# High and low halves of q and k: one full-width copy and one difference, pieces placed by DMA, and later due times for q

## The chip, the cores and the metric

The kernel runs on one core of a Trainium2 chip. Its engines work side by side, each through its own list of instructions: TensorE (PE; its weight loads are shown as PEld), VectorE (DVE), ScalarE (ACT), GpSimd (POOL) and SyncE (SP), which here issues all DMAs. The metric is device time in microseconds; lower is better. A time is the median of several runs; a profile comes from one further execution, whose own time is given beside it.

## The reference

A network of four layers over 1040 tokens (16 meta tokens and 1024 of the input) with 1024 channels, in float32. Layers 0 and 3 are the same kind, sliding-window attention; layer 1 is an mLSTM and layer 2 an HGRN2. Only the attention layers are touched:

```python
def attention_branch(u, w_in, q_gain, k_gain, sinks, w_out, valid, pos):
    q, k, v, z = _split(u @ w_in, (A_W, A_KVW, A_KVW, A_W))
    q = rope(rmsnorm(q.reshape(bsz, lp, A_HEADS, A_HD), q_gain), pos)
    k = rope(rmsnorm(k.reshape(bsz, lp, A_KV, A_HD), k_gain), pos)
    v = v.reshape(bsz, lp, A_KV, A_HD)
    o = sliding_window_attention(q, k, v, sinks, valid)
    return (o * jax.nn.silu(z)) @ w_out

def reference(...):
    for i in range(DEPTH):
        u = rmsnorm(h, norm_gain[i])
        y = attention_branch(...) | mlstm_branch(...) | hgrn2_branch(...)
        h = h + where(valid, y, 0)
```

There are 16 query heads and 4 key heads of 64 channels; a token attends to itself and the 127 before it.

## The kernel before

Activations lie with channels on the 128 partitions and tokens along the free axis. The tokens come in three chunks of 400, 384 and 256 (`CHUNKS`; in layer 3 the first chunk of q is 384 wide, `LAST_CHUNKS`), and the attention in nine blocks, of 16 tokens and then of 128. To keep float32 accuracy with a fast matmul format, each operand is held as two rounded parts, high and low: `h = round(x)`, `l = x - h`. Weights and normed activations take three matmuls for each product (h·h, h·l, l·h).

Two heads share a tile of 128 partitions, 64 each. The scores use that: a q operand (`qs`) of one head has the high part in one half of its 128 partitions and the low part in the other, and k has two operands per head, one with the high part in both halves and one with the low part in both. So two matmuls (lines 621 and 622) give all four products. Building these operands is the split. Before, `k_split` (lines 432 to 451) makes, for each of two heads of a chunk, two copies of the high part (444, 445), one difference (446) and one copy of it (447). `q_split` (lines 453 to 470) makes one copy (463) and one difference (464) for each head. All of these work on 64 partitions, ACT the copies and DVE the differences, and write from one half of the partitions to the other where the operand asks for it.

What precedes a split is in `qk_proj`: the projection of one tile and chunk is 24 matmuls (line 228); `evac` (489) has ACT write the scaled values `dst` (492) and their squares `sq` (493) and has SP issue four DMAs of 32 partitions (496) that put the rotated quarters of `dst` into `rot`. Then come, at due times behind the projection: the rope table (`factors`, 503, one buffer); the statistic, a PE matmul over `sq` (516 for q, 525 for k); the rope itself, `dst*cos + rot*sin` (530 to 532), with the norm factor for k (534); and the split.

There are 8 q tiles per layer, so 8 x 3 splits of q in a layer and 48 in the kernel; there are two k tiles, so 2 x 3 splits of k in a layer, 12 in the kernel. `dst`, `sq` and `rot` of q, and of the second k tile, are three of six shared temporaries (`tmp()`, `TMPS = 6`), which v's evacuation, the gates and the norm units use too; the first k tile uses long rows instead. A temporary comes free when the last instruction or DMA that touches it is done. The norm units (386, 194, 195) make the two parts of the normed activations, tile by tile, ahead of the projections.

PE's order is written out by hand. Every step has a PE cost in ns, and `chain`, `spread` and `weave` merge the projections (fill) with the steps of the attention (S scores, T transposes, V values). The due times `D_K` and `D_Q` are in ns of PE work of the fill after a projection's end: for q the table, the statistic, the rope and the split; for k the statistic, the rope and the split. A step with no PE cost has only a place in the program; the other engines' and SP's lists are made by a scheduler that goes by that order and by what is ready. Each engine works through its list in order, and SP too: a DMA that has to wait for its data keeps back what stands behind it. Weights are loaded ahead by 12000 ns of PE work (`LOOKAHEAD`), into two raw buffers, and split by ACT and DVE (194, 195).

A layer starts with a head: for each chunk the first k tile and q tile 0 (in layer 0 also q tile 1; in layer 3 all three chunks of q tile 1 follow at the end). Then come four segments, one per pair of q tiles, with fill woven in: v and the next pair's q in the first, the second k tile, its v, gates and the last pair's q in the third, which runs 12000 ns (`K_AHEAD`) of fill before its scores. At the end of `layer_a` (748 to 754) a q split that would come before the last scores of the previous pair for its chunk is moved behind them, since `qs` has four buffers per chunk.

Of the kernel before, what the change touches and what calls it, by code (L numbers as in the profile page):

```python
# [9 lines left out]
F32 = mybir.dt.float32  # L10
F32R = mybir.dt.float32r
AF = mybir.ActivationFunctionType
ALU = mybir.AluOpType
PSUM = bass.MemoryType.PSUM

P = 128
# [8 lines left out]
CHUNKS = [(0, 400), (400, 384), (784, 256)]  # L25
# [4 lines left out]
def blk(b):  # L30
    return (0, NMETA) if b == 0 else (NMETA + P * (b - 1), P)
# [15 lines left out]
PARTS = 4  # L47
FIRST = (0.2, 0.8, 0.85), (0.2, 0.75, 0.8)
D_K = 2000.0, 4000.0, 6000.0
D_Q = 1500.0, 2500.0, 3500.0, 4500.0  # L50


MM = 1.0 / 2.4
# [58 lines left out]
def hybrid_kernel(ctx: ExitStack, tc: tile.TileContext, ins, out, layers=(0, 1, 2, 3)):  # L112
    nc = tc.nc
    v, s, g, pe, sp = nc.vector, nc.scalar, nc.gpsimd, nc.tensor, nc.sync
# [11 lines left out]
    def nm(x):  # L126
        ctr[0] += 1
        return f"{x}{ctr[0]}"
# [4 lines left out]
    def rrow():  # L133
        return rpool.tile([P, T], F32R, tag="r", name=nm("r"), bufs=ROWS)
# [16 lines left out]
    def psa():  # L151
        return psum("pa", 1)
# [58 lines left out]
    def proj(src, evac, chunks=CHUNKS):  # L211
        st = {}

        def pre():
            st["w"] = weights(src, "m")

        groups = []
        for n, (c0, cn) in enumerate(chunks):
            grp = []
            for part in range(4):  # L220
                def fn(n=n, c0=c0, cn=cn, part=part):
                    if part == 0:
                        st[n] = psj()
                    h, l = st["w"]
                    acc = st[n]
                    for k in (2 * part, 2 * part + 1):
                        for i, (a, b) in enumerate(((h, uh), (h, ul), (l, uh))):
                            pe.matmul(acc[:, :cn], a[:, k, :], b[:, k, c0 : c0 + cn],  # L228
                                      start=(k == 0 and i == 0), stop=(k == KT - 1 and i == 2))
                    if part == 3:  # L230
                        evac(acc, n, c0, cn)

                grp.append([6 * cn * MM, fn, pre if (n == 0 and part == 0) else None])
            groups.append(grp)
        return groups
# [101 lines left out]
    def rstd_from(acc, dst, cn, n):  # L337
        s.activation(dst[:, :cn], acc[:, :cn], AF.Ln, bias=eps, scale=1.0 / n)
        s.activation(dst[:, :cn], dst[:, :cn], AF.Exp, scale=-0.5)
# [76 lines left out]
    def layer_a(i, j, first, last, fin):  # L416
        win, wout = ins["a_win"][j], ins["a_wout"][j]
        chunks = LAST_CHUNKS if last else CHUNKS
        R = {}
# [9 lines left out]

        order = {}  # L430

        def k_split(j):


            def step(kf, n, c0, cn):
                def fn():
                    if n == 0:
                        R["k", j] = [(rrow(), rrow()) for _ in range(2)]
                    k = kf()
                    cs = slice(c0, c0 + cn)  # L440
                    for hh in range(2):
                        kh, kl = R["k", j][hh]
                        hs, os = slice(64 * hh, 64 * hh + 64), slice(64 - 64 * hh, 128 - 64 * hh)
                        s.copy(kh[hs, cs], k[hs])
                        s.copy(kh[os, cs], k[hs])
                        v.tensor_tensor(kl[hs, cs], k[hs], kh[hs, cs].bitcast(F32), op=ALU.subtract)
                        s.copy(kl[os, cs], kl[hs, cs].bitcast(F32))

                return [0.0, fn, None]

            return step

        def q_split(t):


            def step(qf, n, c0, cn):
                def fn():
                    q = qf()
                    R["q", t, n] = []
                    for hh in range(2):  # L460
                        st = R["mix"].tile([P, CHUNKS[n][1]], F32R, tag=f"qs{n}", name=nm("qs"), bufs=4)
                        hs, os = slice(64 * hh, 64 * hh + 64), slice(64 - 64 * hh, 128 - 64 * hh)
                        s.copy(st[hs, :cn], q[hs])
                        v.tensor_tensor(st[os, :cn], q[hs], st[hs, :cn].bitcast(F32), op=ALU.subtract)  # L464
                        R["q", t, n].append(st)

                order["q", t, n] = z = [0.0, fn, None]
                return z

            return step  # L470
# [15 lines left out]
        def qk_proj(src, gcol, work, fsplit, ch, t=None):  # L486
            late = {}

            def evac(acc, n, c0, cn):
                dst, sq, rot = work(n, c0, cn)  # L490
                late[n] = dst, sq, rot
                s.activation(dst, acc[:, :cn], AF.Identity, scale=R["cons"][:, gcol : gcol + 1])
                s.activation(sq, acc[:, :cn], AF.Square)
                for q in range(4):
                    o = q ^ 1
                    sp.dma_start(rot[32 * q : 32 * q + 32], dst[32 * o : 32 * o + 32])

            def finish(n, c0, cn):
                def factors():
                    b0, bn = CHUNKS[n]  # L500
                    if R.get("cs", (None,))[0] != n:
                        R["cs"] = n, R["mix"].tile([P, 2, 400], F32, tag="cs", name=nm("cs"), bufs=1)
                        sp.dma_start(R["cs"][1][:, :, :bn], ins["rope"][:, :, b0 : b0 + bn].rearrange("a p t -> p a t"))
                    late[n] += (R["cs"][1][:, :, c0 - b0 : c0 - b0 + cn],)

                def stat_q():

                    sq = late[n][1]
                    nb = len(CHUNK_BLOCKS[n])
                    R["rq", t, n] = rq = R["mix"].tile([P, 2 * nb], F32, tag=f"rq{n}", name=nm("rq"), bufs=4)  # L510
                    st = psa()
                    for k, b in enumerate(CHUNK_BLOCKS[n]):
                        if last and b == 0:
                            continue
                        q0 = blk(b)[0] - c0
                        pe.matmul(st[:, 2 * k : 2 * k + 2], sq[:, q0 : q0 + P], R["masks"][:, 0:P:64], start=True, stop=True)
                    z = slice(2 if last and n == 0 else 0, 2 * nb)
                    s.activation(rq[:, z], st[:, z], AF.Ln, bias=eps, scale=1.0 / 64)
                    s.activation(rq[:, z], rq[:, z], AF.Exp, scale=-0.5)

                def stat():
                    factors()
                    sq = late[n][1]
                    st = psa()
                    pe.matmul(st[:, :cn], R["masks"][:, 0:P], sq, start=True, stop=True)
                    rstd_from(st, sq, cn, 64)

                def rope():
                    dst, sq, rot, cos_sin = late[n]
                    v.tensor_tensor(dst, dst, cos_sin[:, 0, :cn], op=ALU.mult)  # L530
                    v.tensor_tensor(rot, rot, cos_sin[:, 1, :cn], op=ALU.mult)
                    v.tensor_tensor(dst, dst, rot, op=ALU.add)
                    if t is None:
                        v.tensor_tensor(dst, dst, sq, op=ALU.mult)

                turn = fsplit(lambda: late[n][0], n, c0, cn)
                if t is not None:
                    return [(D_Q[0], [0.0, factors, None]), (D_Q[1], [108 * len(CHUNK_BLOCKS[n]), stat_q, None]),
                            (D_Q[2], [0.0, rope, None]), (D_Q[3], turn)]
                return [(D_K[0], [4 * cn * MM, stat, None]), (D_K[1], [0.0, rope, None]), (D_K[2], turn)]  # L540

            return proj(src, evac, ch), [finish(n, *c) for n, c in enumerate(ch)]

        def tile_of(groups, events):
# [50 lines left out]
        def mixers():  # L595
# [88 lines left out]
            for k in range(len(units) + V_LAG):  # L684
                seg = units[k]["pair"] if k < len(units) else 4
                for lag, cost, fn in ((V_LAG, 480, V_step), (T_LAG, 432, T_step), (0, 480, S_step)):
                    if 0 <= k - lag < len(units):
# [3 lines left out]
                        if fn is S_step and w["b"] == CHUNK_BLOCKS[w["n"]][-1] and w["hh"]:  # L691
# [4 lines left out]
        oc = {t: proj_out(wout[t - 1], wout[t], lambda k, t=t: R["o", t - 1 + k], chunks,  # L696
                          fin if t == 7 else None, t == 5) for t in (1, 3, 5, 7)}
        kg0, kfin0 = qk_proj(win[0], 1, work_rows(3), k_split(0), CHUNKS)
        kg1, kfin1 = qk_proj(win[1], 1, tmps, k_split(1), CHUNKS)
        vg0, vfin0 = v_proj(win[2], 0)  # L700
        vg1, vfin1 = v_proj(win[3], 1)
# [46 lines left out]
        for i in range(3, 12):  # L748
            for t in (2 * (i // 3), 2 * (i // 3) + 1):
                at = [id(z) for z in body]  # L750
                q, k = (at.index(id(z)) if id(z) in at else -1
                        for z in (order["q", t, i % 3], order["S", i // 3 - 1, i % 3]))
# [579 lines left out]
    for pos, i in enumerate(layers):  # L1332
# [10 lines left out]
        if i % 3 == 0:  # L1343
            head, body, oa, ob = layer_a(i, i // 3, tail is None, i == 3, fin)
        elif i % 3 == 1:
            head, body, oa, ob = layer_b(i, i // 3, fin)
        else:
            head, body, oa, ob = layer_c(i, i // 3, fin)
# [27 lines left out]
    ahead, k = 0.0, 0  # L1376
# [6 lines left out]
    k = 0  # L1383
# [120 lines left out]
```

## Time and profile before

| | us |
|---|---|
| median of 3 runs | 2632.33 |
| lowest, highest run | 2629.12, 2633.46 |
| the profiled execution: its time | 2634.16 |
| its span, first to last instruction | 2632.4 |
| POOL busy in the span | 249.6 |
| mean granted TensorE clock | 0.992 |

The span is the stretch that all positions below refer to, counted from its start. A row of a window lists the busy time of the engines with the number of instructions, the clock that was granted to PE, the mean busy share of the DMA engines, and GB/s. A row of a timeline is start, duration, engine, line, operation, what it writes and reads, its shape, how many are merged in the row, and in brackets the idle time before it and what ended that. A row of a group or of a line gives the count, the durations and the idle time ahead of it. SPq is SP's list, where the duration of a DMA is the time that its issue took, not the transfer.

### The profile page before, as it was taken

What the parts mean: (1) busy time and instruction counts of PE and PEld (TensorE: products, weight loads), DVE (VectorE), ACT (ScalarE), POOL (GpSimd) and SP (SyncE); (2) the same over time, 40 slices, a digit from 0 to 9 for tenths busy, and PEclk for the clock granted to TensorE, in tenths of its full rate; (3) what the DMA queues carried; (4) which work ended last, traced back from release to release, by engine and by line L of the source; (5) the groups of instructions that cost most, each with busy time, mean ns of one, the idle gap of its engine ahead of it and who ended that gap; (6) DMA issues with size and microseconds to landing.
All of it is one profiled execution on the core that took longest, in us unless ns stands there. A gap on an engine that the chain in (4) does not pass through costs nothing.

```text
span 2632.4 us, 54257 instructions
## 1 busy us (share of the span) xinstructions
PE 2570.6 (98%) x20422; PEld 2488.0 (95%) x20422; DVE 1976.7 (75%) x5296; ACT 1667.5 (63%) x4374; POOL 249.6 (9%) x502
## 2 busy tenths in 40 slices
PE   7999999989999999999999999999999999999999
PEld 5999989989999999999999999999999998999999
DVE  6797788784747474747475688989887978887996
ACT  6676767565454545454545757878685857767772
POOL 2221231000000000000000000100000000321330
PEclk9999999999999999999999999999999999999999
DMA  4212111011111111111111101111110113212112
GB/s 130 67 50 84 54 44 47 21 63 52 41 57 41 57 41 57 41 53 45 53 45 49 53 30 42 34 35 34 35 41 30 38 50 90 58 46 84 55 38 80
DMA packets 82583, 135.92 MB, mean 52 GB/s; under 512 B 12033, under 2 KB 35713, under 8 KB 82321
## 3 DMA queue, kind: packets, MB, share of 16 engines
q1 hardware_dynamic: 82320, 132.45, 15.7%
q8 instruction: 161, 2.64, 0.4%
q14 instruction: 102, 0.83, 0.1%
HBM read 117.56 MB, written 4.26 MB: 46 GB/s over the span
## 4 chain that ended last, share of the span: by engine, by line
PE 76%; DVE 12%; ACT 7%; issue 2%; DMA 2%; POOL 1%; SPq 0%; DVEq 0%; ACTq 0%; POOLq 0%
PE pj L228 36%; PE pj L322 16%; PE pj L277 10%; PE po L666 2%; PE pt L647 1%; ACT Sm L632 1%; PE po L910 1%; PE pa L924 1%; DVE wl L195 1%; PE po L912 1%; DVE Sm L629 1%; PE pj L273 1%; DVE qs L464 1%; DVE Pl L650 1%; PE pm L1162 1%
## 5 line engine op out<-in xcount | busy, mean ns | idle before, releaser
L228 PE MATMUL pj<-uh,wh 128*128 128x256 f32 (+2 forms) x2688 | 917.8, 341 | 8.4 <-ACT uh L194 8.4
L228 PE MATMUL pj<-ul,wh 128*128 128x256 f32 (+2 forms) x2688 | 868.8, 323 | 3.7 <-DVE ul L195 3.5
L228 PE MATMUL pj<-uh,wl 128*128 128x256 f32 (+2 forms) x2688 | 866.4, 322 | 0.0
L228 PEld LDWEIGHTS pj<-uh,wh 128*128 128x128 f32 x2688 | 511.4, 190 | 25.3 <-ACT uh L194 11.6
L228 PEld LDWEIGHTS pj<-ul,wh 128*128 128x128 f32 x2688 | 511.6, 190 | 12.5 <-DVE ul L195 7.4
L228 PEld LDWEIGHTS pj<-uh,wl 128*128 128x128 f32 x2688 | 510.8, 190 | 0.0
L194 ACT CAST wh<-wr 128x512 fp32r<-128x512 f32 (+1 forms) x338 | 203.3, 613 | 110.2 <-PE pj L322 31.2
L195 DVE TENSOR_TENSOR wl<-wr,wh 128x512 fp32r<-128x512 f32 (+1 forms) x338 | 233.9, 701 | 51.9 <-ACT wh L194 49.4
L322 PE MATMUL pj<-yh,wh 128*128 128x384 f32 (+2 forms) x768 | 254.2, 331 | 9.0 <-DVE x L325 6.6
L325 DVE TENSOR_TENSOR x<-x,pj 128x384 f32<-128x384 f32 (+2 forms) x480 | 234.9, 508 | 34.5 <-PE pj L322 33.0
L322 PE MATMUL pj<-yl,wh 128*128 128x384 f32 (+2 forms) x768 | 246.3, 321 | 0.0
L322 PE MATMUL pj<-yh,wl 128*128 128x384 f32 (+2 forms) x768 | 246.2, 321 | 0.0
L277 PE MATMUL pj<-wh,uh 128*128 128x256 f32 (+1 forms) x768 | 232.2, 302 | 0.0
L277 PE MATMUL pj<-wl,uh 128*128 128x256 f32 (+1 forms) x768 | 216.8, 282 | 0.0
L277 PE MATMUL pj<-wh,ul 128*128 128x256 f32 (+1 forms) x768 | 216.4, 282 | 0.0
L635 POOL TENSOR_TENSOR Sm<-Sm,s 128x512 f32<-128x512 f32 (+2 forms) x136 | 141.3, 1039 | 459.6 <-DVE s L634 450.2
L632 ACT ACTIVATE Sm<-Sm,s 128x257 f32<-128x257 f32 (+2 forms) x272 | 131.0, 483 | 83.0 <-DVE s L629 79.9
L404 ACT ACTIVATE t<-t 128x384 f32<-128x384 f32 (+2 forms) x240 | 117.9, 491 | 86.8 <-DVE t L403 85.2
L403 DVE SCALAR_TENSOR_TENSOR t<-pj,t 128x384 f32<-128x384 f32 (+2 forms) x192 | 98.9, 515 | 79.5 <-ACT t L402 77.5
L322 PEld LDWEIGHTS pj<-yh,wh 128*128 128x128 f32 x768 | 145.1, 189 | 13.6 <-DVE x L325 8.5
L194 ACT CAST yh<-r 128x384 fp32r<-128x384 f32 (+2 forms) x120 | 57.1, 478 | 149.4 <-PE pj L322 137.3
L277 PEld LDWEIGHTS pj<-wh,uh 128*128 128x128 f32 x768 | 144.7, 188 | 2.1
(255 smaller groups left out, 5438.3 us busy)
## 6 DMA issues: line engine op xcount, KB each, us to landing
wr<-in_b_win SPq DMA_DIRECT2D x124, 256.0 KB, 2.8
wr<-in_a_win SPq DMA_DIRECT2D x80, 256.0 KB, 2.8
wr<-in_c_win SPq DMA_DIRECT2D x64, 256.0 KB, 2.7
wr<-in_a_wout SPq DMA_DIRECT2D x32, 256.0 KB, 2.8
wr<-in_b_wout SPq DMA_DIRECT2D x32, 256.0 KB, 2.7
t<-t SPq DMA_DIRECT2D x104, 48.0 KB, 1.9
cs<-in_rope SPq DMA_DIRECT2D x11, 400.0 KB, 3.3
cs<-in_rope SPq DMA_DIRECT2D x11, 384.0 KB, 3.2
```

Source lines behind the costliest of these rows:

```text
L194: s.copy(h, src)
L195: v.tensor_tensor(l, src, h.bitcast(F32), op=ALU.subtract)
L228: pe.matmul(acc[:, :cn], a[:, k, :], b[:, k, c0 : c0 + cn], start=(k == 0 and i == 0), stop=(k == KT - 1 and i == 2))
L273: pe.matmul(acc[:48, :nc], um[0][:, k, :], m[:, kk, :], start=(k == 0 and m is wh), stop=(k == KT - 1 and m is wl))
L277: pe.matmul(acc[:cn, :nc], a[:, k, c0 : c0 + cn], m[:, kk, :], start=(k == 0 and j == 0), stop=(k == KT - 1 and j == 2))
L322: pe.matmul(acc[:, :cn], a[:, k, mc], b, start=(k == 0 and i == 0), stop=(k == 1 and i == 2))
L325: v.tensor_tensor(x[:, m, c0 : c0 + cn], x[:, m, c0 : c0 + cn], acc[:, :cn], op=ALU.add)
L403: v.scalar_tensor_tensor(a[:, :cn], z, 0.0, a[:, :cn], op0=ALU.min, op1=ALU.subtract)
L404: s.activation(a[:, :cn], a[:, :cn], AF.Exp)
L632: s.activation(Sm[:nq, u, : nk + 1], Sm[:nq, u, : nk + 1], AF.Exp, scale=-1.0, bias=st[:nq, u : u + 1], accum_out=den[:nq, u : u + 1])
L635: g.tensor_tensor(Sm[:nq, :, :nk], Sm[:nq, :, :nk], den[:nq].rearrange("p (u c) -> p u c", c=1).to_broadcast([nq, 2, nk]), op=ALU.mult)
L666: pe.matmul(po[:, :, q0 - g0 : q0 - g0 + nq], V[pair // 2, kb][:kn, P * hh : P * hh + P], w[part][:kn, ki, :, :nq], start=(ki == 0 and par ...
```

## The change

`halves` makes both parts over all 128 partitions: the high part is written over `rot` by one ACT copy, the low part over `dst` by one DVE difference. Each piece of 64 partitions then goes to its place by a DMA from SP: eight for a chunk of k (two parts, two heads, two halves of the operand), four for a chunk of q (two parts, two heads). The due times of q go from 1500, 2500, 3500 and 4500 to 2000, 3000, 4000 and 6000. Those of k, the number of temporaries and all else stay.

```diff
-D_Q = 1500.0, 2500.0, 3500.0, 4500.0
+D_Q = 2000.0, 3000.0, 4000.0, 6000.0
...
+        def halves(src, rot):
+
+            hi_, lo_ = rot.bitcast(F32R), src.bitcast(F32R)
+            s.copy(hi_, src)
+            v.tensor_tensor(lo_, src, rot, op=ALU.subtract)
+            return hi_, lo_
+
...
-                    k = kf()
                     cs = slice(c0, c0 + cn)
-                    for hh in range(2):
-                        kh, kl = R["k", j][hh]
-                        hs, os = slice(64 * hh, 64 * hh + 64), slice(64 - 64 * hh, 128 - 64 * hh)
-                        s.copy(kh[hs, cs], k[hs])
-                        s.copy(kh[os, cs], k[hs])
-                        v.tensor_tensor(kl[hs, cs], k[hs], kh[hs, cs].bitcast(F32), op=ALU.subtract)
-                        s.copy(kl[os, cs], kl[hs, cs].bitcast(F32))
+                    for i, z in enumerate(halves(*kf())):
+                        for hh in range(2):
+                            for o in range(2):
+                                sp.dma_start(R["k", j][hh][i][64 * o : 64 * o + 64, cs].bitcast(F32),
+                                             z[64 * hh : 64 * hh + 64].bitcast(F32))
...
-                    q = qf()
-                    R["q", t, n] = []
-                    for hh in range(2):
-                        st = R["mix"].tile([P, CHUNKS[n][1]], F32R, tag=f"qs{n}", name=nm("qs"), bufs=4)
-                        hs, os = slice(64 * hh, 64 * hh + 64), slice(64 - 64 * hh, 128 - 64 * hh)
-                        s.copy(st[hs, :cn], q[hs])
-                        v.tensor_tensor(st[os, :cn], q[hs], st[hs, :cn].bitcast(F32), op=ALU.subtract)
-                        R["q", t, n].append(st)
+                    R["q", t, n] = [R["mix"].tile([P, CHUNKS[n][1]], F32R, tag=f"qs{n}", name=nm("qs"), bufs=4)
+                                    for _ in range(2)]
+                    for i, z in enumerate(halves(*qf())):
+                        for hh, st in enumerate(R["q", t, n]):
+                            sp.dma_start(st[64 * i : 64 * i + 64, :cn].bitcast(F32), z[64 * hh : 64 * hh + 64].bitcast(F32))
...
-                turn = fsplit(lambda: late[n][0], n, c0, cn)
+                turn = fsplit(lambda: (late[n][0], late[n][2]), n, c0, cn)
```

## Prediction

> **What bounds the kernel now.** I read the page first, then windows over the two attention layers (layer 0, about 20 to 445 us, and layer 3, about 2183 to 2570 us; the change touches nothing else), then the groups of the lines that change, then single timelines.
>
> ```profile
> span 2632.4 us, 54257 instructions
> PE 2570.6 (98%) x20422; PEld 2488.0 (95%) x20422; DVE 1976.7 (75%) x5296; ACT 1667.5 (63%) x4374; POOL 249.6 (9%) x502
> ```
>
> PE is busy 98% of the span and its order is fixed by the program, so any wait that the change puts on PE's path is paid in full, and work taken off DVE and ACT is worth only what it removes of PE's idle time or of its slow clock. The windows say how much there is (columns: busy us and instruction count of PE, weight loads, DVE, ACT, POOL, then granted clock, DMA share, GB/s):
>
> ```profile
> 43.00:95.00 52.00, 43.16 (x226) 38.84 (x227) 35.88 (x89) 35.50 (x99) 8.41 (x13) 0.80 0.21 61
> 260.00:445.00 185.00, 180.60 (x1246) 173.66 (x1245) 155.11 (x419) 137.76 (x391) 45.72 (x73) 0.99 0.16 50
> 2204.00:2215.00 11.00, 9.54 (x44) 8.27 (x42) 8.81 (x18) 6.13 (x16) 0.00 (x0) 0.69 0.28 84
> 2235.00:2395.00 160.00, 155.41 (x1096) 152.40 (x1095) 140.99 (x361) 113.53 (x325) 41.47 (x63) 1.00 0.20 61
> 2405.00:2570.00 165.00, 159.79 (x1114) 155.95 (x1113) 141.83 (x367) 122.68 (x339) 43.63 (x64) 0.99 0.16 50
> 361.00:364.00 3.00, 3.00 (x13) 2.51 (x12) 1.94 (x5) 1.11 (x7) 0.32 (x2) 0.50 0.00 0
> ```
>
> PE loses 8.8 us of idle and about 10 us of clock (52 x 0.20) in layer 0's head, 1.5 and 3.4 us (11 x 0.31) in layer 3's, and 4.4, 4.6 and 5.2 us in the bodies. The last row is what follows a PE wait: 3 us at clock 0.50, 1.5 us of work lost.
>
> **What is removed.** Durations from the groups:
>
> ```profile
> L463 ACT CAST qs<-t 64x384 fp32r<-64x384 f32 (+2 forms) x96 | 45.7, 476 | 12.4 <-DVE t L532 11.1
> L464 DVE TENSOR_TENSOR qs<-t,qs 64x384 fp32r<-64x384 f32 (+2 forms) x96 | 56.5, 588 | 14.7 <-ACT qs L463 12.2
> L447 ACT CAST r<-r 64x400 fp32r<-64x400 f32 (+2 forms) x24 | 11.5, 479 | 0.9 <-DVE r L446 0.5
> L446 DVE TENSOR_TENSOR r<-r,r 64x400 fp32r<-64x400 f32 (+2 forms) x12 | 6.6, 546 | 3.2 <-ACT r L444 2.9
> L194 ACT CAST yh<-r 128x384 fp32r<-128x384 f32 (+2 forms) x120 | 57.1, 478 | 149.4 <-PE pj L322 137.3
> ```
>
> A 128-partition cast costs what a 64-partition one does (478 and 476 ns), so one replaces two without growing. The 48 q steps each lose one copy (48 x 0.476 = 22.8 us of ACT) and one difference (48 x 0.588 = 28.2 us of DVE). The 12 k steps go from six copies to one (60 x 0.479 = 28.7 us of ACT) and lose one difference (12 x 0.546 = 6.6 us). Together 51.5 us of ACT and 34.8 us of DVE, beside a PE that is busy 97 to 98% in the bodies.
>
> Where it can pay is the heads, where the last norm units of a chunk (lines 386, 194, 195) queue among the k copies. In layer 3's head that wait and the half clock behind it are 4.9 us; I do not count them as a gain, because the next stop there is later still (below). In layer 0's head I take 3 us, nearest to k's five copies there (5 x 0.479 = 2.4); bounds: a gain of 8, and a loss of 3 if the longer held buffers starve the norm units. In the bodies I take 2 us of the 14.2 idle; bounds 0 and 5.
>
> **What is added.** Four DMAs per q step, eight per k step: 192 + 96 = 288, all on SP's queue. No 64-partition copy within on-chip memory is in this trace; the nearest row is the 32-partition one of the rotation, line 496; the loads of line 206 are the low end.
>
> ```profile
> L496 SPq DMA_DIRECT2D t<-t x216: 507/588/1716, 29.9 to 2486.2; - x108
> DMA to landing us min/median/max: 1.8/1.9/4.3
> L206 SPq DMA_DIRECT2D wr<-in_a_win x80: 327/328/1023, 5.0 to 2536.4; - x80
> ```
>
> Four rotations take 2.41 us of SP (rows below), 0.60 each with the gap. Bounds: 0.33 (the load), 1.2 (twice the rotation, if the cost goes with the partitions). I take 0.60: 173 us of SP in all, and 4 x 0.60 + 1.9 = 4.3 us from a copied q to its last landing. The Trainium skill, page "DMA: Bandwidth & Descriptors", section "Issuing engines are not separate DMA queues", says that the sequencer's time to start a DMA is usually small beside the DMA. By it SP would not be a place to wait, which is rival B below; here four issues outlast a landing (2.41 against 1.9 us).
>
> A split's DMA also waits in SP's queue for the copy or the difference, and what stands behind it is rotations, rope tables (line 503) and weight loads. Weight loads are issued 12000 ns of PE work ahead, which covers a few us.
>
> **Layer 3's head, where the queue overflows.** SP's timeline, with the last difference of q tile 1, chunk 0, and the first score matmul:
>
> ```profile
> 2198.26 2.41 SPq L496 DMA_DIRECT2D r<-r  x4
> 2201.10 1.61 SPq L206 DMA_DIRECT2D wr<-in_a_win  x2
> 2206.59 0.38 SPq L503 DMA_DIRECT2D cs<-in_rope  x1
> 2207.06 2.41 SPq L496 DMA_DIRECT2D t<-t  x4
> 2209.57 2.44 SPq L496 DMA_DIRECT2D r<-r  x4
> 2215.37 2.41 SPq L496 DMA_DIRECT2D t<-t  x4
> 2217.87 0.53 SPq L503 DMA_DIRECT2D cs<-in_rope  x1
> 2218.45 0.95 SPq L206 DMA_DIRECT2D wr<-in_a_win  x2
> 2221.20 2.42 SPq L496 DMA_DIRECT2D t<-t  x4
> 2223.73 0.52 SPq L503 DMA_DIRECT2D cs<-in_rope  x1
> 2224.34 1.41 SPq L206 DMA_DIRECT2D wr<-in_a_win  x2
> 2227.07 2.98 SPq L496 DMA_DIRECT2D t<-t  x4
> ```
>
> ```profile
> 2229.46 1.14 DVE L464 TENSOR_TENSOR qs<-t,qs 64x384 fp32r<-64x384 f32 x2
> 2234.23 0.28 PE L621 MATMUL pm<-r,qs 128*128 128x256 f32 x1
> ```
>
> The first score product needs q tiles 0 and 1 of chunk 0; the last piece is ready at 2230.60, 3.6 us early. In the program's order the turns of k chunks 0 to 2 and of q tile 0, chunks 0 to 2, come before that of q tile 1, chunk 0: in PE ns of the head's last part, which runs k chunk 2, q0 chunk 2, then q1 chunks 0, 1, 2 (2560, 2560, 3840, 3840, 2560), k1 is due at 2160, q0 chunk 1 at 6000, k2 at 8560, q0 chunk 2 at 11120, and q1 chunk 0 at 8960 + 6000 = 14960 (13460 before). So SP has to issue 3 x 8 + 4 x 4 = 40 new DMAs, 24 us, beside the rows shown after the first, 18.1 us (17.5 with the last at 2.41). From 2200.67 that is 2242.2, landed 2244.1: PE waits 9.9 us. At 0.33 us each the queue ends at 2231.4 and lands at 2233.3: nothing. At 1.2 it is 34 us. I take 10. Both orders of the queue among the 40 give the same end. Layer 0 has the same issues, but its scores start from tiles of chunk 0 copied thirty us earlier, so there only slack is used up.
>
> **The second k projection, where buffers run out.** There (line 699) k works in the six shared temporaries, three per chunk, three chunks in a row. Layer 3, then layer 0:
>
> ```profile
> 2399.88 0.47 ACT L492 ACTIVATE t<-pj,cons 128x256 f32<-128x256 f32 x1 [1.16 <-DMA t<-t]
> 2399.90 0.58 DVE L534 TENSOR_TENSOR t<-t,t 128x400 f32<-128x400 f32 x1
> 2400.51 0.39 ACT L493 ACTIVATE t<-pj 128x256 f32<-128x256 f32 x1 [0.16 <-DVE t L534]
> 2400.95 0.70 PE L525 MATMUL pa<-t,masks 128*128 128x256 f32 x2
> ```
>
> ```profile
> 255.09 0.57 DVE L534 TENSOR_TENSOR t<-t,t 128x400 f32<-128x400 f32 x1
> 256.24 0.38 ACT L493 ACTIVATE t<-pj 128x256 f32<-128x256 f32 x1
> 256.67 0.70 PE L525 MATMUL pa<-t,masks 128*128 128x256 f32 x2 [0.94 <-ACT t L493]
> ```
>
> Chunk 2's two evacuations take two buffers of chunk 0 as these come free, the rotated one after its sum (line 532) and the square after line 534; PE's statistic waits for the second. After the change the rotated buffer holds the high half until its four DMAs have landed. From the end of line 534 that is copy 0.5 + 4 x 0.60 + 1.9 = 4.8 us, then the square, 0.4: 2405.7 in place of 2400.9, and 260.9 in place of 256.6. k's due times stay, so PE's statistic does not move back: +4.8 and +4.3 us. Low end, with 0.33 issues: 3.7 and 3.2. High end 8 each, if the last q tiles ahead of k free their buffers late too. I take 4.8 twice.
>
> **Elsewhere.** In the bodies the evacuations of two q tiles in a row, and the end of the first one's split, are these:
>
> ```profile
> 211.05 0.60 ACT L492 ACTIVATE t<-pj,cons 128x400 f32<-128x400 f32 x1
> 218.20 0.59 ACT L492 ACTIVATE t<-pj,cons 128x400 f32<-128x400 f32 x1 [0.21 <-PE pj L228]
> ...
> 220.11 1.51 DVE L464 TENSOR_TENSOR qs<-t,qs 64x400 fp32r<-64x400 f32 x2 [0.64 <-ACT qs L463]
> ```
>
> A q comes every 7 us and lives 10.6 us in its buffers. With 4.3 more it lives 15, two at a time in six buffers, and the square, free after the statistic, gives the third its place: nothing, bounds 0 and 12 (36 body tiles, a third of a us each). Each of three new PE waits brings a spell of half clock at 1.5 us: 4.5, bounds 0 and 10.
>
> **Sum.** -3 - 2 + 10 + 4.8 + 4.8 + 4.5 = +19 us, on the profiled execution's 2634.2 (span 2632.4, so 1.8 around it), 2653; against the runs' median, 2632.3, it is **2651**.
>
> **Rivals.** B, cheap issue: DMAs at 0.33, no queue in layer 3's head; left are 3.5 twice, one spell of 1.5 each, minus 3 and 2: +5, **2637**. For it: the 328 ns row; against: rotation, the same kind of copy, at 588.
> C, faster: in both heads ACT and DVE are the gate before PE, and the removed copies open it; the norm units come early and the half clock there goes. Priced 8 us in layer 0, 4.9 in layer 3, 5 in the bodies, less 7 for the second k: -11, **2621**. It decides if q tile 1 lands before about 2234, that is if the 40 DMAs cost under 0.35 us each or the small pieces needed last go out first. For it: 43 to 95 us at clock 0.80; against: SP's rows.
> D, issue by the partition, 1.2 us: +34 in that head, 7 for each second k, queues in the bodies 10, less 5, plus 6 of clock: +59, **2691**.
> E, the splits don't matter (all landings covered, gains too small to see): **2632**. Against: the square's wait is direct.
>
> **Chances.** About 0.2%, 5 us, can be told from no change. Forecast 0.50; B 0.14, split between same and slower; C 0.19; D 0.07; E 0.10, some of it a small loss or gain. Slower 0.50 + 0.07 (D) + 0.07 (half of B) + 0.04 (of E) = 0.68; same 0.07 + 0.05 = 0.12; faster 0.19 + 0.01 = 0.20. The forecast's own range is 2640 to 2670 (head 3 to 20, second k 3.5 to 8 each); taking in E, B and most of C below and leaving D out, 2622 to 2676.
>
> **What would show it.** Right: score matmuls of line 621 early in layer 3 waiting for DMA into q's tiles; line 525 of the second k's third chunk idle 4 to 5 us for line 493, which waits for a DMA out of the temporaries; SP without a gap from about 2200 to 2240; half clock after each. Wrong: split issues near 330 ns, line 525 on time, or clock 1.0 through both heads.

## The result, and the profile after

| | before | after |
|---|---|---|
| median of 4 runs each, us | 2631.18 | 2663.26 |
| lowest, highest | 2629.12, 2633.46 | 2660.67, 2666.74 |
| the profiled execution: time | 2634.16 | 2660.67 |
| its span | 2632.4 | 2658.9 |
| mean granted TensorE clock | 0.992 | 0.985 |

Before has one run more here than in the table ahead of the prediction. The changed kernel is slower: ratio 1.0124, 95% interval 1.0112 to 1.0137, 32 us on the medians. The profiles show 26.5 us of it, because the profile of before comes from an execution of 2634.16 us, above all of its four runs, and that of after from its shortest run.

The page of after, its span and engine rows:

```profile
span 2658.9 us, 54736 instructions
...
PE 2574.5 (97%) x20422; PEld 2495.2 (94%) x20422; DVE 1934.9 (73%) x5236; ACT 1617.4 (61%) x4266; POOL 245.7 (9%) x502
```

ACT lost 50.1 us of work (1667.5 to 1617.4) and DVE 41.8 (1976.7 to 1934.9), against the 51.5 and 34.8 worked out from the diff, and the kernel is slower all the same. PE does the same 20422 matmuls with 3.9 us more of busy time, so most of the loss is PE idle. The page does not say where; the waits of PE do (line and what it waited for, us in total, times, longest). Before, the waits of the statistics for a square of ACT were short, and no score product waited for a DMA:

```profile
PE pa L525 <- ACT t L493: 0.9, 1, 0.9
...
PE pa L516 <- ACT t L493: 0.2, 1, 0.2
```

After, lines behind the split have a number one higher: 525 is now 526, 516 is 517, 621 is 622, 493 is 494.

```profile
PE pa L526 <- ACT t L494: 16.6, 6, 4.3
PE pa L517 <- ACT t L494: 13.7, 2, 7.3
...
PE pm L622 <- DMA qs<-t: 5.4, 1, 5.4
```

35.7 us in three lines: the statistic of k (526) and that of q (517), both late for a square of ACT (494), and a score product late for a DMA into q's tiles. The windows of after in the two heads, two as before, then two new ones in layer 3's head, the second of them at half clock:

```profile
43.00:95.00 52.00, 46.89 (x255) 43.25 (x256) 30.38 (x85) 26.63 (x84) 8.15 (x14) 0.80 0.46 115
2204.00:2215.00 11.00, 10.82 (x78) 10.23 (x77) 8.69 (x20) 6.70 (x18) 0.00 (x0) 1.00 0.64 170
2212.00:2253.00 41.00, 24.34 (x135) 23.27 (x133) 11.81 (x25) 9.52 (x28) 0.00 (x0) 0.79 0.48 126
2243.50:2259.50 16.00, 7.77 (x27) 7.49 (x28) 6.77 (x16) 4.71 (x13) 0.77 (x1) 0.50 0.52 149
```

Between 2212 and 2253 us PE, DVE, ACT and POOL are all idle for long: PE works 24.3 of 41 us, ACT 9.5, DVE 11.8. When no engine works for long, look at the queue that feeds them. SP's list in that stretch, whole from 2212.36 to 2252.96:

```profile
2212.36 2.54 SPq L466 DMA_DIRECT2D qs<-t  x4
2214.96 2.49 SPq L497 DMA_DIRECT2D t<-t  x4
2217.49 2.49 SPq L497 DMA_DIRECT2D r<-r  x4
2220.08 5.74 SPq L450 DMA_DIRECT2D r<-r  x8
2225.86 2.50 SPq L497 DMA_DIRECT2D t<-t  x4
2228.46 0.53 SPq L504 DMA_DIRECT2D cs<-in_rope  x1
2229.09 2.42 SPq L466 DMA_DIRECT2D qs<-t  x4
2231.56 0.58 SPq L206 DMA_DIRECT2D wr<-in_a_win  x1
2232.25 2.44 SPq L497 DMA_DIRECT2D t<-t  x4
2234.79 5.01 SPq L450 DMA_DIRECT2D r<-r  x8
2239.85 0.59 SPq L504 DMA_DIRECT2D cs<-in_rope  x1
2240.53 2.38 SPq L466 DMA_DIRECT2D qs<-t  x4
2243.01 6.85 SPq L497 DMA_DIRECT2D t<-t  x8
2249.96 0.53 SPq L504 DMA_DIRECT2D cs<-in_rope  x1
2250.53 2.43 SPq L466 DMA_DIRECT2D qs<-t  x4
```

Start plus duration of each row is, to about 0.1 us, the start of the next: SP issues for 40 us with one gap, inside the row of eight rotations at 2243.01, which takes 6.85 us where two rows of four take 4.9. The timeline of the other engines there shows what this holds up (in brackets the idle time before, and its releaser):

```profile
2232.42 0.58 ACT L493 ACTIVATE t<-pj,cons 128x384 f32<-128x384 f32 x1 [8.41 <-DMA qs<-t]
...
2234.76 1.44 PE L517 MATMUL pa<-masks,t 128*128 128x2 f32 x6 [7.26 <-ACT t L494]
...
2244.34 0.47 ACT L493 ACTIVATE t<-pj,cons 128x256 f32<-128x256 f32 x1 [7.23 <-DMA qs<-t]
...
2246.37 1.01 PE L517 MATMUL pa<-masks,t 128*128 128x2 f32 x4 [6.41 <-ACT t L494]
...
2249.38 0.41 PE L622 MATMUL pm<-r,qs 128*128 128x256 f32 x1
...
2255.37 0.55 PE L622 MATMUL pm<-r,qs 128*128 128x256 f32 x1 [5.36 <-DMA qs<-t]
```

ACT cannot evacuate q's projection (493), because the temporary that it would write is held by a split's DMA into `qs` (8.41 and 7.23 us); that DMA stands in SP's queue. PE's statistic (517) waits for the square behind that evacuation, twice, 7.26 and 6.41 us; only then comes the wait for a landing in front of the second score product, 5.36 us. The queue makes its own delay longer: the rotations of the late evacuations go out only from 2243.01, behind the splits, SP's one gap is a wait for such an evacuation (2244.34), and the split that the second score product waits for goes out only at 2250.53.

The second k of layer 3, from the same kind of timeline:

```profile
2421.50 0.49 ACT L494 ACTIVATE t<-pj 128x384 f32<-128x384 f32 x1 [3.81 <-DMA qs<-t]
2421.99 0.57 DVE L535 TENSOR_TENSOR t<-t,t 128x400 f32<-128x400 f32 x1
...
2422.77 2.47 SPq L497 DMA_DIRECT2D t<-t  x4
2423.03 0.47 ACT L493 ACTIVATE t<-pj,cons 128x256 f32<-128x256 f32 x1
...
2425.28 4.48 SPq L450 DMA_DIRECT2D r<-t  x7
...
2428.44 0.56 DVE L535 TENSOR_TENSOR t<-t,t 128x384 f32<-128x384 f32 x1
2429.03 0.38 ACT L494 ACTIVATE t<-pj 128x256 f32<-128x256 f32 x1 [3.33 <-DVE t L535]
...
2429.47 0.70 PE L526 MATMUL pa<-t,masks 128*128 128x256 f32 x2 [4.33 <-ACT t L494]
```

Chunk 2's evacuation (2423.03) takes the square's buffer of chunk 0, free after line 535 at 2421.99. Its own square needs one more. The other two buffers of chunk 0 are held by eight DMAs that SP starts at 2425.28, behind a rotation (2422.77); so it takes the square's buffer of chunk 1, free after 2428.44 + 0.56. From chunk 0's line 535 to the statistic is 7.5 us, where from line 534 it was 1.05 before (2399.90 to 2400.95). One chunk earlier a buffer is held by a DMA into `qs`, of the q tile ahead of k (3.81 at 2421.50), and PE's statistics of the first two chunks wait 1.87 and 2.17 us. Layer 0 has the same pair of rows 8.4 us apart, 1.6 before (255.09 to 256.67), and its first two chunks wait 0.95 and 3.20 us:

```profile
255.33 0.57 DVE L535 TENSOR_TENSOR t<-t,t 128x400 f32<-128x400 f32 x1
...
263.77 1.22 PE L526 MATMUL pa<-t,masks 128*128 128x256 f32 x2 [4.07 <-ACT t L494]
```

To sum this up, the starts of the same matmul in two traces were subtracted (scores: 621 or 622; statistic of k: 525 or 526). The first column is its position before; the others tell how much later (or earlier) it stands, in us. The kernels are those of the next section.

```
                            before  after  later-q  old-q    q     k    POOL
layer 0, end of pair 1       233.0   -2.9    -2.7    5.5    2.0   0.3    0.3
layer 0, 1st score, pair 2   272.3    9.2    -2.9   17.0    7.0   5.7   10.4
layer 2, end                2182.2    4.3    -1.4   10.5    3.5   4.4    6.6
layer 3, 1st score          2234.2   15.2    -6.1   22.5    4.4   3.8    9.7
layer 3, 5th unit of scores 2261.4   22.1    -1.3   27.5   12.4   8.1   12.5
layer 3, end of pair 1      2377.6   19.6    -3.7   23.9   10.2   8.0   13.6
layer 3, 1st score, pair 2  2419.4   29.0    -3.3   33.4   13.0  13.5   22.8
end of span                 2632.4   26.5    -5.4   32.2    7.3  13.5   21.0
```

After loses 12.1 us at layer 0's second k (-2.9 to 9.2), 17.8 in layer 3's head (4.3 to 22.1), 9.4 at layer 3's second k (19.6 to 29.0), and gets some us back in the stretches between. Single profiles are good to some 5 us here: two kernels below, with one half each of the step in the due times, end 5.7 and 6.5 us earlier in this count and are level with before in their medians. The three losses are above that, and the changed kernel with the old due times (old-q) repeats them: 11.5, 17.0 and 9.5 us.

### The profile page after: what moved, and what is told of

The parts are those of the page before. It is cut to its first block, busy times and chain, and to the rows that moved or that the text cites. A ratio compares the mean times of both kernels' runs of the same rounds, so it can differ in the third digit from the quotient of the medians.

```text
span 2658.9 us, 54736 instructions
## 1 busy us (share of the span) xinstructions
PE 2574.5 (97%) x20422; PEld 2495.2 (94%) x20422; DVE 1934.9 (73%) x5236; ACT 1617.4 (61%) x4266; POOL 245.7 (9%) x502
## 4 chain that ended last, share of the span: by engine, by line
PE 80%; DVE 8%; ACT 4%; DMA 3%; issue 2%; SPq 2%; POOL 1%; DVEq 0%; ACTq 0%; POOLq 0%
PE pj L228 39%; PE pj L322 15%; PE pj L277 10%; PE po L667 2%; PE pt L648 2%; PE po L911 1%; PE pa L925 1%; PE po L913 1%; SPq L497 1%; PE pm L622 1%; PE pa L517 1%; PE pm L623 1%; PE pj L273 1%; PE pm L1163 1%; DVE wl L195 1%
## 5 line engine op out<-in xcount | busy, mean ns | idle before, releaser
L228 PEld LDWEIGHTS pj<-uh,wh 128*128 128x128 f32 x2688 | 513.3, 191 | 24.7 <-ACT uh L194 10.8
```

Of the source, the lines that this page charges most:

```text
L228: pe.matmul(acc[:, :cn], a[:, k, :], b[:, k, c0 : c0 + cn], start=(k == 0 and i == 0), stop=(k == KT - 1 and i == 2))
```

## The experiments

Ratios are against runs of the kernel before on the same chip, with 95% intervals. Before had medians of 2629.68, 2629.49 and 2628.2 us in the three batches.

**The due times alone: the kernel before with the new due times of q.**

```diff
-D_Q = 1500.0, 2500.0, 3500.0, 4500.0
+D_Q = 2000.0, 3000.0, 4000.0, 6000.0
```

> The kernel before with the later due times of q alone, no DMA in the splits. Theory 1 (SP's queue and the held temporaries cost the time): the due times alone cost little, 2631 to 2636 us, and in layer 3's head the third to sixth q evacuations stay on time. Rival (the later due times are what starves the first scores and the temporaries): most of the +27 of the profiled span is there, 2650 or more.

2625.67 us, ratio 0.9983 (0.9974 to 0.9992). The later due times help a little on their own, so the whole loss and more belongs to the new splits.

**The new splits alone: the changed kernel with the old due times.**

```diff
-D_Q = 2000.0, 3000.0, 4000.0, 6000.0
+D_Q = 1500.0, 2500.0, 3500.0, 4500.0
```

> The changed kernel with the old due times of q. Theory 1: within 4 us of the changed kernel, 2659 to 2667 us, for SP issues the same 288 DMAs and the buffers are held to the landing. Rival (due times): back to 2636 or less.

2668.22 us, ratio 1.0150 (1.0135 to 1.0165). The due times are worth 5 us here (2668.22 less 2663.26, from two batches) and 4 without the DMAs. In layer 0's head this kernel stands at +5.5, the one with the due times alone at -2.7 and after at -2.9: the copies that were removed show no gain there.

**Only q by DMA**, k split as before, new due times:

```diff
-                    for i, z in enumerate(halves(*kf())):
...
+                    k = kf()[0]
+                    for hh in range(2):
...
+                        s.copy(kh[hs, cs], k[hs])
+                        s.copy(kh[os, cs], k[hs])
+                        v.tensor_tensor(kl[hs, cs], k[hs], kh[hs, cs].bitcast(F32), op=ALU.subtract)
+                        s.copy(kl[os, cs], kl[hs, cs].bitcast(F32))
```

> Only q's splits by DMA (192 DMAs), with the new due times; k's splits as before. Theory 1: the second k projection frees its buffers as before except for those that q holds ahead of it, so its stages lose 0 to 4 us each in place of 12 and 9; layer 3's head issues 16 new DMAs in place of 40, 9.6 us in place of 24, and its wait falls from about 18 to 0 to 6 us. In all 2632 to 2642 us. If the loss is DMA landing latency of q before the scores, and not the queue, the head still loses 10 or more: 2645 to 2652.

2636.99 us, ratio 1.0034 (1.0021 to 1.0047). Its waits of PE (lines stand three lower than in after):

```profile
PE pa L529 <- ACT t L497: 7.9, 4, 3.1
PE pm L625 <- DMA qs<-t: 6.4, 1, 6.4
...
PE pa L520 <- ACT t L497: 3.0, 1, 3.0
```

All three waits of after are there. With part of the head's DMAs gone from its queue SP is late for the score product as in after (6.4 us, one time), but less for the statistic of q (3.0 in place of 13.7). The head loses 8.9 us (3.5 to 12.4), more than the 0 to 6 expected. The second k waits 7.9 us though none of its own pieces goes by DMA: in both layers it is the first two chunks that wait (4.1 us in layer 0, 3.8 in layer 3), for temporaries that q's DMAs hold; the third does not wait.

**Only k by DMA**, q split as before, old due times:

```diff
...
-                    for i, z in enumerate(halves(*qf())):
...
+                    q = qf()[0]
+                    R["q", t, n] = []
+                    for hh in range(2):
...
+                        s.copy(st[hs, :cn], q[hs])
+                        v.tensor_tensor(st[os, :cn], q[hs], st[hs, :cn].bitcast(F32), op=ALU.subtract)
```

> Only k's splits by DMA (96 DMAs), q's splits and due times as before. Theory 1: the second k's statistic still waits for the landing of the high half, 4 to 6 us in both attention layers; layer 3's head has 24 new issues, 14 us, which the 3.6 us of slack and SP's idle take up to 0 to 6 us late. In all 2640 to 2650 us, and with the run of q alone this adds to less than the whole change, because the queue overflows only with both.

2647.12 us, ratio 1.0064 (1.0047 to 1.0080). Only the second k waits for long, and the head loses 3.7 us (4.4 to 8.1) in place of 17.8:

```profile
PE pa L529 <- ACT t L497: 9.0, 2, 4.8
...
2412.77 0.39 ACT L497 ACTIVATE t<-pj 128x256 f32<-128x256 f32 x1 [2.41 <-DVE t L538]
...
2413.21 1.22 PE L529 MATMUL pa<-t,masks 128*128 128x256 f32 x2 [4.18 <-ACT t L497]
```

Here it is the third chunk that waits, 4.8 us in layer 0 and 4.2 in layer 3 (the rows), and its square is released by DVE (line 538, 535 in after), as in after. So of after's 16.6 us at the second k about half is k's own and half is that of the q tiles ahead of it.

The two parts add up to 7.3 + 17.4 = 24.7 us, after loses 32. The excess of 7 fits a queue that overflows only when both are in it; the intervals of the two ratios, 0.0013 and 0.0017 to each side (3.4 and 4.5 us), leave it barely resolved. In the table it lies in layer 3's head, 17.8 us against 8.9 and 3.7.

**The split's DMAs issued by POOL:**

```diff
-                                sp.dma_start(R["k", j][hh][i][64 * o : 64 * o + 64, cs].bitcast(F32),
+                                g.dma_start(R["k", j][hh][i][64 * o : 64 * o + 64, cs].bitcast(F32),
...
-                            sp.dma_start(st[64 * i : 64 * i + 64, :cn].bitcast(F32), z[64 * hh : 64 * hh + 64].bitcast(F32))
+                            g.dma_start(st[64 * i : 64 * i + 64, :cn].bitcast(F32), z[64 * hh : 64 * hh + 64].bitcast(F32))
```

> The changed kernel with the 288 new DMAs issued by POOL, not SP; the buffers are held to the landing as before. Theory 1 (two separate costs: SP's issue queue in layer 3's head, held temporaries at the second k): layer 3's head loses 0 to 8 us in place of 18, SP has gaps there; the second k still loses 5 to 12 us in each attention layer, for the landing is no earlier. In all 2640 to 2650 us. Rival 2 (buffers alone make both): the head stays at 12 us or more and the time at 2655 or more. Rival 3 (the queue alone makes both): the second k's waits go too, 2630 or less.

2655.68 us, ratio 1.0097 (1.0082 to 1.0112).

```profile
PE pa L526 <- ACT t L494: 15.1, 4, 8.1
...
PE pa L364 <- POOL r L356: 6.9, 2, 5.3
PE pa L517 <- ACT t L494: 6.9, 1, 6.9
```

In layer 3's head the loss falls from 17.8 to 5.9 us (6.6 to 12.5); one of the two waits of line 517 is gone, and what is left of the wait for a landing before the scores is 1.6 us. The second k waits nearly as long as in after, 15.1 against 16.6 us. So SP's queue makes most of the head's loss and little or none of the second k's. The time is above the 2640 to 2650 expected. One reason is a price of POOL's own: a norm statistic in layer 0's head (364) now waits 5.3 us for POOL's sum (356), a wait that is 1.6 us in after.

**Eight temporaries instead of six**, to tell the buffers from the queue. They were given room by two rows of `YS` in place of three, which itself costs time, so the kernel before was run with the same sizes as its control.

```diff
-ROWS, TMPS, RAWS, YS = 8, 6, 2, 3
+ROWS, TMPS, RAWS, YS = 8, 8, 2, 2
```

The control, the kernel before:

> Control: the kernel before with eight temporaries and two y buffers, no other change. Two y buffers may cost 0 to 10 us in the out projections of all four layers, eight temporaries may give back 1 to 3 us at the second k: 2628 to 2640 us.

2671.26 us, ratio 1.0159 (1.0144 to 1.0175), far above the 2628 to 2640 expected. At the end of layer 2 it is 31.4 us behind before (2213.6 against 2182.2), through the output projections of the first three layers (line 322), which wait for their operands (16.3 us in all four layers). Only differences from it are used.

The changed kernel with eight temporaries:

> The changed kernel with eight shared temporaries in place of six, and two y buffers in place of three to make room. Theory 1: against the kernel before with the same buffers, the second k's statistic waits fall from 12 and 9 us to 0 to 3 each; in layer 3's head the waits of the statistics for the squares go, but the first scores still wait for the queue, 8 to 12 us. In all 10 to 16 us above that control. Rival 2 (buffers alone): level with the control. Rival 3 (queue alone): as far above the control as the change is above before, 28 or more.

2699.93 us, ratio 1.0267 (1.0252 to 1.0283): 28.7 over its control. Its waits:

```profile
PE pm L622 <- DMA qs<-t: 11.7, 1, 11.7
...
PE pj L228 <- ACT wh L194: 5.7, 1, 5.7
...
PE pa L526 <- ACT t L494: 2.4, 2, 1.6
```

The wait of the second k is nearly gone, 2.4 in place of 16.6 us, and that of line 517 has left the list. But the total has hardly come down: SP's queue is as long, and what PE saved in the head at the statistic of q it now waits for before the score, 11.7 in place of 5.4, and once, 5.7 us, for the high half of a weight, whose cast stands in ACT's list behind a split's copy. In shifts against the control, the head loses 20.3 us (4.7 to 25.0) and the second k 4.0 and 4.1 in place of 12.1 and 9.4. The 28.7 us are not the 10 to 16 expected; as a time they are what rival 3, the queue alone, had named, and only the waits and shifts at the second k speak against it.

**Both: eight temporaries and POOL.**

```diff
-ROWS, TMPS, RAWS, YS = 8, 6, 2, 3
+ROWS, TMPS, RAWS, YS = 8, 8, 2, 2
...
-                                sp.dma_start(R["k", j][hh][i][64 * o : 64 * o + 64, cs].bitcast(F32),
+                                g.dma_start(R["k", j][hh][i][64 * o : 64 * o + 64, cs].bitcast(F32),
...
-                            sp.dma_start(st[64 * i : 64 * i + 64, :cn].bitcast(F32), z[64 * hh : 64 * hh + 64].bitcast(F32))
+                            g.dma_start(st[64 * i : 64 * i + 64, :cn].bitcast(F32), z[64 * hh : 64 * hh + 64].bitcast(F32))
```

> The changed kernel with eight temporaries, two y buffers, and the new DMAs from POOL. Theory 1: both costs go; what is left of the landing is covered by the due times: within 6 us of the control with the same buffers. If it stays 10 or more above that control, a third cost is at work (POOL's own waits, or the landing before the first scores).

2676.84 us, ratio 1.0180 (1.0161 to 1.0199): 5.6 over its control. Of the three waits one is left that is above 2 us:

```profile
PE pm L622 <- DMA qs<-t: 6.1, 1, 6.1
```

The four kernels make a square. Loss against the kernel before with the same number of temporaries, in us of the medians:

| | 6 temporaries | 8 temporaries |
|---|---|---|
| SP issues | 32.1 | 28.7 |
| POOL issues | 26.2 | 5.6 |

By the scatter of the runs each figure is good to some 3 to 6 us. Neither cure does much alone, both together take 26.5 of 32.1 us. This fits two causes in series on PE's path, each of which hides part of the other.

**What is in the due times.** First half of the step, the table and the statistic later; second half, the rope and the split later; and all of it later still. All three are the kernel before with one line changed:

```diff
-D_Q = 1500.0, 2500.0, 3500.0, 4500.0
+D_Q = 2000.0, 3000.0, 3500.0, 4500.0
```

> The kernel before with only the table and the statistic of q later (2000, 3000, 3500, 4500). The later due times together gave 4 us, most of it in layer 3's head (-3.9 us between the end of layer 2 and the last k statistic of the head, where the granted clock went from 0.69 to 1.00). Theory: the gain comes from q's rope and split, 4 ACT copies and DVE steps that stand ahead of the norm units; then this kernel gains little, within 1.5 us of before, and the clock between 2204 and 2215 us stays near 0.7. Rival: the gain comes from PE reaching the statistic of q later, past the ACT square; then this kernel gains 3 to 4 us.

```diff
-D_Q = 1500.0, 2500.0, 3500.0, 4500.0
+D_Q = 1500.0, 2500.0, 4000.0, 6000.0
```

> The kernel before with only the rope and the split of q later (1500, 2500, 4000, 6000). Theory (rope and split stand ahead of the norm units): 3 to 4 us faster than before, clock near 1.0 between 2204 and 2215 us. Rival (the statistic): within 1.5 us of before.

```diff
-D_Q = 1500.0, 2500.0, 3500.0, 4500.0
+D_Q = 2500.0, 4000.0, 6000.0, 9000.0
```

> The kernel before with all due times of q later still (2500, 4000, 6000, 9000). Theory: the heads' gain is used up at the first step (the clock there is already 1.0), and the last q tiles come later for their scores, so this is 0 to 4 us slower than with the change's due times. Rival: the gain goes on, 2 us or more faster than with the change's due times (below 0.9976 of before).

2627.91 us, 0.9999 (0.9990 to 1.0008); 2627.96 us, 0.9999 (0.9990 to 1.0008); 2621.42 us, 0.9974 (0.9965 to 0.9983). The theory fell in all three, though the first kernel's time lies where it had put it: neither half of the step gains anything, and later still gains most. So does the reading on which it was built. The first half shows the better clock between 2204 and 2215 us, 1.00 in place of 0.69, and is not faster:

```profile
2204.00:2215.00 11.00, 10.83 (x73) 10.41 (x73) 8.97 (x18) 8.67 (x22) 0.00 (x0) 1.00 0.40 113
```

What makes the longest due times 6.8 us faster stays open. This last kernel, without any DMA for the splits, is the fastest of all that ran.

## Why the prediction was right, and where its sizes were off

The direction, the two places and the two causes (SP's queue and held temporaries) were right, and the time lies in the forecast's own range of 2640 to 2670. The loss was 32 us in place of 19: the term of layer 3's head was too small, and at the second k one part was left out of the sum, while the part that was sized right came by another path.

- **Removed work.** The durations were right, and so was that PE would not feel it: the lines of the splits lost 51.5 us on ACT and 34.2 on DVE, and most of the rest of DVE's 41.8 is in the first multiply of the rope, for a reason that is not known. The -3 for layer 0's head has no support: the kernel with the due times alone stands there as after does (-2.7 and -2.9), and such a shift is within what profiles of kernels of equal time differ by. Nor can the bodies' -2 be told: after gets back 2.5 us behind layer 3's head and behind its second k (22.1 to 19.6; 29.0 to 26.5), but the kernel with the due times alone, where no copy was removed, gets back 2.4 and 2.1 there (-1.3 to -3.7; -3.3 to -5.4).
- **Price of an issue.** The trace of after has k's issues and landings like the first rows; the last is q's issues by POOL in the kernel that used it:

```profile
L450 SPq DMA_DIRECT2D r<-r x48: 464/595/1315, 43.2 to 2239.2; - x48
...
DMA to landing us min/median/max: 1.9/2.2/4.0
```

```profile
L466 POOL DMA_DIRECT2D qs<-t x192: 516/523/572, 47.6 to 2527.7; - x192
```

  The forecast's 0.60 holds. That rules out rival B (0.33) and rival D (1.2, by the partition). The Trainium skill, page "DMA: Bandwidth & Descriptors", section "Issuing engines are not separate DMA queues", has the sequencer's time as usually small beside the DMA. By this trace it is a quarter for one DMA (0.6 us against a landing of 2.2), but it adds up where many small DMAs meet: four issues take 2.4 us, the forty of layer 3's head some 25, and the queue decides.
- **Layer 3's head: +10 forecast, 17.8 measured.** This term was mis-sized. Its end of the queue was worked out from the instructions in it, as if their data were always ready: the last piece issued at 2242.2, against 2252.96 (2250.53 + 2.43) in the trace. Of these 10.8 us, 4.3 are the lateness with which layer 3 begins, 2.4 one rotation of four more than had been counted ahead of that piece, and some 2 the gap. What was left out is that the queue's DMAs hold temporaries. ACT's evacuations wait for these (8.41 and 7.23 us), the statistic waits for ACT, PE stops, and the next rotations reach SP later. The forecast saw one wait, before the scores, and there were three (7.26, 6.41 and 5.36 us); with POOL issuing, the head loses 5.9.
- **Second k: +4.8 forecast for each, 12.1 and 9.4 measured.** That held temporaries are the cause is shown: with two more buffers the wait for the square falls from 16.6 to 2.4 us in all. The forecast had only the third chunk wait, and that wait has its size: 4.07 and 4.33 us in after, 4.8 and 4.2 with k alone by DMA. But the size came out by luck, for the step "the end of line 534, then copy, four issues and a landing" is not what happens. SP first issues the next chunk's rotation, 2.47 us, which had been left out, so the buffers of chunk 0 come free later still, and the square takes one of chunk 1, released by DVE, at about that time; from line 535 (534 before) to the statistic the time grew by 6.4 us, and in layer 0 by 6.9. What was not in the sum is the first two chunks, which wait 4.2 us in layer 0 and 4.0 in layer 3, because q tiles ahead of k hold their buffers late (3.81 us at 2421.50); with q alone by DMA just these waits are there. That had been given as the high end, 8 us, and both losses are above it.
- **Half clock: 4.5 forecast.** The waits of over 4 us are followed by it, as expected; those of 1.87 and 2.17 us in layer 3 are not. In the head it lasts 16 us (clock 0.50 from 2243.5 to 2259.5), not 3, as one wait follows another; PE is busy for 7.77 us of that, so it costs up to 3.9 there, and it is included in the sizes above.
- **The named signs.** Score products waiting for DMA into q's tiles: one, 5.36 us. Line 526 of the third chunk: 4.33 us idle for line 494, but 494 is released by DVE's line 535 and not by a DMA, as the buffer is another one. SP without a gap: from 2212 to 2253 but for some 2 us, forecast 2200 to 2240.
- **Rival C, faster,** hung on issues under 0.35 us or on the ordering of the queue; neither holds. **Rival E** is excluded by the waits.

Not tried: the split's DMAs with another order in SP's queue, and fewer of them, with both halves of an operand of k filled by one DMA.

## What to carry to other kernels

Copies that are moved from an engine to DMAs move to the queue that issues them: count that queue's time (here 0.6 us each) in the densest stretch, not its mean over the kernel. A buffer that a DMA reads is held until the landing, and that landing stands behind everything ahead of it in the queue; where buffers and queue are both short, size the two together, since here each cure alone left most of the loss (26.2 and 28.7 of 32.1 us). Before explaining a shift of a few microseconds between two profiles, see whether a kernel with the same median shows it too.

## What was not expected of the hardware

The issue of an on-chip copy takes as long for 64 partitions (0.595 us median for k, 0.548 for q) as for 32 (0.588), and longer than that of a weight load from outside of 256 KB (0.328). POOL's issues of q are even, 0.516 to 0.572 us, where those on SP range from 0.461 to 1.754 in this row of after:

```profile
L466 SPq DMA_DIRECT2D qs<-t x192: 461/548/1754, 48.3 to 2531.8; - x192
```
